# A gMLP layer in fp32 on one core: second half of x loaded two steps later, weights fetched ahead of parts of h, one emptying of a queue removed

## The chip, the cores and the metric

The kernel runs on one core of one Trainium2 chip. The metric is device microseconds of that core for the whole program. A run is repeated, and the median of the repeats is shown; the profile is of one more execution, whose own time is given beside its span.

## The reference

With DEPTH = 1 only the first mixer runs, a gated MLP with a spatial mixing over chunks of 128 positions. x is 1024 x 2048, `w_in` is 2048 x 12288, `w_out` is 4096 x 2048, all float32.

```python
h = rmsnorm(x, a_norm)
z = h @ w_in                                   # 1024 x 12288
u, v, gate = jnp.split(z, 3, axis=-1)          # 4096 columns each
u = gelu(u)
v = rmsnorm(gelu(v), v_gain)
sv = einsum('gpq,nqgc->npgc', w_s, v) + b_s    # 8 groups of 512 columns, chunks of 128 rows
y = u * sv
x = x + (y * silu(gate)) @ w_out
return rmsnorm(x, final_norm)
```

## The kernel before

**Arithmetic.** Every matrix product keeps float32 accuracy with a fast matmul type: a matrix is split into a high and a low part (`split`, L90: ACT copies the high part `w_hi`, L92; DVE subtracts it to get the low part `w_lo`, L93), and each product is the sum of three matmuls (`mm3`, L104: high by high L106, high by low L107, low by high L108). The big products are cut into 2 x 2 blocks and computed with seven block products in place of eight (`A_OF`, `B_OF`, L20); many of these need the sum or difference of two weight blocks, a `w_sum` that DVE makes (`combine`, L116).

**Strips and steps.** The input projection goes over 12 strips of 1024 columns (four of v, then eight that pair 512 columns of u with the same of the gate), then the output projection follows. The program is one list of steps (L124 to L129), each some 24 matmuls of 128 x 128 by 512. Strip 0 makes h from x itself and writes its parts to DRAM; all others read these parts of h back. From strip 2 on, strips come in pairs, and products 2 and 5 of a pair are cut once more by the same scheme: these "deep" steps have 12 matmuls, read the parts `d_1h` to `d_7l`, and come first in each pair (`deep_stage`, L504). There are five such stages, at strips 2, 4, 6, 8 and 10.

**What is fetched when.** At the start of step i, `advance` (L491) calls `prefetch` for the steps up to LOADS = 3 steps ahead (a deep step counts half) and then `feed` for step i + 2, which makes the `w_sum` and the split on DVE and ACT. `prefetch` (L176) loads a step's weight blocks (`load_w`, issued at L156, tile `w_raw`) and behind them its two parts of h (L191, tiles `a_hi` and `a_lo`). All of these go through the one queue of SP, in program order, 512 KB each; a load waits there until its slot in a pool of 21 ("big") is free. In strip 0, `first_step` (L315) loads the second half of x (`load_x`, L287, tile `x_t`) in the same queue, one of eight blocks in each of the steps 2 to 9. POOL's queue writes the parts of h to DRAM and moves v and y.

**Small work between steps.** What has to be done to a finished product (activations on ACT, the multiplication by the gain on DVE, L351, and so on) is put in two lists, `soon` and `later`. `work(us)` (L262) takes from them after each step, as far as a budget goes. `work_all` (L268) empties both; it is called at the end of strip 1 (L677), when the last products of that strip are in the lists, and in the deep stage of strip 4 (L528).

Engines execute their own instructions in program order, so a `w_sum` that waits for its weights holds up every DVE instruction behind it.

Of the kernel before, what the change touches and what calls it, by code (L numbers as in the profile page):

```python
# [7 lines left out]
F32 = mybir.dt.float32  # L8
F32R = mybir.dt.float32r
# [27 lines left out]
def gmlp_kernel(ctx, tc, x, xT, g_in, w_in, gain, wsT, bsT, w_out, fnorm, out):  # L37
    nc = tc.nc
# [12 lines left out]
    AHEAD, LOADS = 2, 3  # L51
# [7 lines left out]
    def slot(tag, name, dt=F32):  # L59
        return main.tile([P, 2, C], dt, tag=tag, name=name, bufs=SLOTS[tag])  # L60

    def bank_set(n, name):

        return [ps.tile([P, 2, 512], F32, tag=f"set{n}_{t}", name=f"{name}_{t}") for t in range(2)]
# [59 lines left out]
    steps = [("in", s, p, j) for s in range(2) for p in (IN_ORDER if s else FIRST_ORDER) for j in range(JI)]  # L124
    for s in range(2, len(strips), 2):
# [7 lines left out]
    a_dram = {(p, j): [dram.tile([P, 2, HT], F32, tag=f"a{p}_{j}{l}", name=f"a{p}_{j}{l}") for l in "hl"]  # L133
              for p in IN_ORDER for j in range(JI)}

    d_dram = {(p, q): [dram.tile([P, 2, C], F32, tag=f"d{p}_{q}{l}", name=f"d{p}_{q}{l}") for l in "hl"]
              for p in DEEP for q in IN_ORDER}

    wraw, yraw, wparts, aparts = {}, {}, {}, {}
    hx = {}  # L140

    def load_w(step, block, us=None):
        kind, s, p, j = step
        mat, cols, n = (w_out, outs, JO) if kind == "out" else (w_in, strips, JI)

        key = (kind, s, 0 if kind == "in" and not (s > 1 and (p, block) == (6, 11)) else p, block, j)
        if key not in wraw or us is not None:
            k = ((block // 10 - 1) * n + j) * 2 * P
            col = cols[s][block % 10 - 1]
            if key not in wraw:  # L150
                wraw[key] = slot("big", "w_raw")

            order = "(p u) c -> p u c" if kind == "out" else "(u p) c -> p u c"
            src = mat[k:k + 2 * P, col:col + C].rearrange(order, p=P)
            us = slice(0, 2) if us is None else us
            nc.sync.dma_start(out=wraw[key][:, us], in_=src[:, us])  # L156
        return wraw[key]

    def load_deep(step, block):

        _, s, (p, q), j = step
        return load_w(("deep", s + block % 10 - 1, p, 2 * (block // 10 - 1) + j), 11 if p == 2 else 22)

    def load_y(step, block):
        _, _, p, j = step
        key = (p, block, j)
        if key not in yraw:
            g, b = divmod(((block % 10 - 1) * JO + j) * 2, CB)
            if g == G - 1 and halves_of_y[0] < 2 * G:
                work_all()  # L170
            yraw[key] = slot("big", "y_raw")
            nc.gpsimd.dma_start(
                out=yraw[key], in_=y_dram[g][block // 10 - 1][b * P:(b + 2) * P].rearrange("(p u) t -> p u t", p=P))
        return yraw[key]

    def prefetch(i):  # L176
        if i >= len(steps):
            return
        kind, s, p, j = step = steps[i]
        if kind == "deep":  # L180
            for block in B_OF[p[1]][::2]:
                load_deep(step, block)
        else:
            for block in B_OF[p][::2]:
                load_w(step, block)
        if kind == "deep" and j > 0:
            aparts[i] = aparts[i - 1]
        elif kind == "deep" or (kind == "in" and s > 0):
            parts = [slot("big", f"a_{l}", F32R) for l in ("hi", "lo")]
            for t, d in zip(parts, d_dram[p] if kind == "deep" else a_dram[p, j]):  # L190
                nc.sync.dma_start(out=t.bitcast(F32), in_=d)  # L191
            aparts[i] = parts
        if kind == "out" and s == 0:
            for block in A_OF[p][::2]:
                load_y(step, block)
# [66 lines left out]
    def work(us=2.3):  # L262
        while soon or (later and us > 0):
            cost, what = (soon or later).pop(0)
            us -= cost
            what()

    def work_all():  # L268
        while soon or later:
            work(1e9)  # L270
# [6 lines left out]
        out=eye, in_=ones[:, 0, :P], pattern=[[-1, P]], compare_op=ALU.is_equal, fill=0.0, base=0, channel_multiplier=1)  # L277
# [3 lines left out]
    def load_x(jj, h, us=None):  # L281

        if (jj, h) not in hx:
            hx[jj, h] = slot("ax" if h == 1 and jj >= JI else "big", "x_t")
        src = xT[jj * 2 * P:(jj + 1) * 2 * P, h * HT:(h + 1) * HT].rearrange("(u p) c -> p u c", p=P)
        us = slice(0, 2) if us is None else us
        nc.sync.dma_start(out=hx[jj, h][:, us], in_=src[:, us])  # L287

    def square_x(jj, h):

        sq = slot("ax", "sq_x")
        nc.scalar.activation(out=sq, in_=hx[jj, h], func=AF.Square)
        if h in sums:
            nc.vector.tensor_tensor(out=sums[h], in0=sums[h], in1=sq, op=ALU.add)
        else:
            sums[h] = sq
# [17 lines left out]

    def first_step(i):  # L315

        if 2 <= i < 10:
            load_x(i - 2, 1)
        if i == 4:
            nc.gpsimd.dma_start(out=ws_sb, in_=wsT.rearrange("g q p -> q g p"))  # L320
        if 1 <= i < 17:
            h, n = divmod(i - 1, 8)
            square_x(order_x[n] if h == 0 else n, h)
        if i in (9, 17):
            scale_x(i // 10)
        if i in (10, 20):

            for t in range(2):
                later.append((0, lambda t=t, act=waiting[i // 10]: act(t)))
# [9 lines left out]
    for j in range(1, JI):  # L339
        load_x(j, 0)  # L340
        load_x(JI + j, 0)
        if j < LOADS:
            prefetch(j)
# [57 lines left out]
    def spatial_step(k, g, cs, n_set):  # L401

        for c, at in enumerate((0, 1, 4, 5)):
            if k == at:
                load_v(g, c)
        for c, at in enumerate((2, 3, 6, 7)):
            if k == at:
                prepare_spatial(g, c)
        if k in (6, 10):
            work(0)  # L410
            half = k // 10
            apply_spatial(g, half, n_set[half], cs[11 + 10 * half])
# [73 lines left out]
    when = [0.0]  # L486
    for step in steps:
        when.append(when[-1] + (0.5 if step[0] == "deep" else 1.0))
    fetched, fed = [LOADS], [AHEAD]

    def advance(i):  # L491
        while fetched[0] < len(steps) and when[fetched[0]] <= when[i] + LOADS:
            prefetch(fetched[0])
            fetched[0] += 1
        feed(i + AHEAD)
# [5 lines left out]
    i = 0  # L501
    deep = {}
# [43 lines left out]
    for s in range(len(strips)):  # L546
# [7 lines left out]
        if is_v:  # L554
            gains = slot("ax", "gain_b")
            load_gains = lambda s=s, gains=gains: nc.gpsimd.dma_start(
                out=gains.rearrange("p a b -> p (a b)"),
                in_=gain[:, 2 * s * C:2 * (s + 1) * C].broadcast_to([P, 2 * C]))
# [90 lines left out]
        for p in FIRST_ORDER if s == 0 else IN_ORDER if s == 1 else REST_ORDER:  # L649
            fresh = p in (1, 2, 5) or (s > 1 and p in (4, 3))  # L650
            if s == 0:
                work(0)
            if fresh:
                second = (1,) if s == 0 else (2,) if s == 1 else (4,)
                sets[p] = bank_set(b if p in second else a, f"m{p}")
            chain = sets[p if fresh else {4: 2, 7: 2, 3: 5, 6: 5}[p] if s < 2 else {7: 4, 6: 3}[p]]
            for j in range(JI):
                advance(i)
                if is_v and (p, j) == (3, 0):
                    load_gains()  # L660
                if not is_v and p in (7, 6):
                    spatial_step(j if p == 7 else 4 + j, *mixing)
                elif p == 1 and s > NV and s % 2:
                    spatial_step(8 + j, *before)
                products(i, chain, fresh)
                if s == 1 and p in DEEP:
                    whole(i)
                if s == 0:
                    first_step(i)
                work(2.3 if s else 1.4)  # L670
                i += 1
            end_of(p, chain)
            if s == 1 and p in DEEP:
                for q in IN_ORDER:
                    later.append((2.3, lambda p=p, q=q: deep_parts(p, q)))
            if s == 1 and p == 6:
                work_all()  # L677
        before = mixing


# [60 lines left out]
    for p in OUT_ORDER:  # L741
        for s in range(len(outs)):
# [3 lines left out]
            for j in range(JO):  # L746
                if j == JO // 2:
                    for block, _ in TO_C[p]:
                        init_acc(s, block)
                    if p == OUT_ORDER[-2] and s == 1:  # L750
                        for n in range(2):
                            fn_b.append(slot("ax", f"fn_b{n}"))
                            nc.gpsimd.dma_start(
                                out=fn_b[n].rearrange("p a b -> p (a b)"),
                                in_=fnorm[:, 2 * n * C:2 * (n + 1) * C].broadcast_to([P, 2 * C]))
# [16 lines left out]
            if last:  # L772

                work_all()
                for m in range(HCH):
# [3 lines left out]
                    d = acc[s, block][m // 2][:, m % 2]  # L779
# [53 lines left out]
```

## Time and profile before

| | |
|---|---|
| median of 3 runs | 2497.97 us (2497.07 to 2501.28) |
| profiled execution, own time | 2498.71 us |
| its span | 2497.0 us |
| mean granted TensorE clock | 0.995 |
| PE busy | 2442.9 us, 98% of the span, 10708 matmuls |
| DVE busy | 1831.9 us, 73%, 1847 instructions |
| ACT busy | 986.1 us, 39%, 1236 instructions |
| DMA | 752.24 MB, mean 301 GB/s |
| loads of `w_in` blocks, 512 KB each | 311, median 7.1 us from issue to landing |

TensorE (PE) is busy nearly all the time, so what can be won is in the short stretches where it is not. The profile cuts the span into 40 slices of 62.4 us, a digit for the busy tenths of each; most digits of PE are 9. Behind it stand views of any stretch: counts and busy time by window, the instructions of one engine in order, the chain of waits, and what each engine waited for. SP and POOL only issue transfers here: "SPq" rows are issues, not the transfers themselves.

### The profile page before, as it was taken

The numbers are of one execution on the slowest core, as the hardware profiler recorded it, in microseconds if no ns is written. First come the engines' busy times: TensorE is split into PE (matmuls) and PEld (weight loads), VectorE is DVE, ScalarE is ACT, GpSimd is POOL, SyncE is SP. The second block draws the span as 40 slices with busy tenths as digits, with TensorE's granted clock in tenths as the row PEclk, the third lists the DMA queues.
The fourth block names the chain that finished last, engine by engine and source line by source line (L and its number), as shares of the span: only waits on it lengthen the run. The fifth ranks groups of instructions, "written<-read, shape, count | busy, mean of one in ns | idle before, by whom it ended". The sixth has DMA issues, their size and how long they took to land.

```text
span 2497.0 us, 29261 instructions
## 1 busy us (share of the span) xinstructions
PE 2442.9 (98%) x10708; PEld 2012.3 (81%) x10708; DVE 1831.9 (73%) x1847; ACT 986.1 (39%) x1236; POOL 234.8 (9%) x414
## 2 busy tenths in 40 slices
PE   8999979999999999999999999999999999999998
PEld 6778868888888887888878888788888888888886
DVE  6996768667876778867788677876777564676795
ACT  5853444333533344343443433434342332232343
POOL 2221100000000101001010010100102110010010
PEclk9999989999999999999999999999999999999999
DMA  9788898899988787897888878888798865678885
GB/s 381 269 335 284 329 381 328 291 346 341 345 311 333 271 328 286 310 340 272 335 288 296 334 278 320 300 304 328 280 339 301 303 221 187 215 275 279 303 278 204
DMA packets 276720, 752.24 MB, mean 301 GB/s; under 512 B 24784, under 2 KB 24800, under 8 KB 276576
## 3 DMA queue, kind: packets, MB, share of 16 engines
q1 hardware_dynamic: 231920, 593.57, 66.7%
q0 software_dynamic: 44656, 156.80, 16.6%
q8 instruction: 85, 1.39, 0.2%
q14 instruction: 59, 0.48, 0.1%
HBM read 664.29 MB, written 85.98 MB: 300 GB/s over the span
## 4 chain that ended last, share of the span: by engine, by line
PE 85%; DMA 7%; DVE 4%; issue 2%; ACT 1%; SPq 1%; POOL 0%; POOLq 0%; ACTq 0%; DVEq 0%
PE m L107 16%; PE m L108 16%; PE m L106 16%; PE o L107 7%; PE o L106 7%; PE o L108 7%; DMA w_raw<-in_w_in 5%; PE d L107 4%; PE d L108 4%; PE d L106 4%; DMA a_lo<-a_2l 1%; DVE w_lo L93 1%; DVE w_sum L116 1%; DMA x_t<-in_xT 1%; PE sv L107 1%
## 5 line engine op out<-in xcount | busy, mean ns | idle before, releaser
L92 ACT ACTIVATE w_hi<-w_sum 128x1024 fp32r<-128x1024 f32 x420 | 444.9, 1060 | 1068.8 <-PE m L107 645.7
L106 PE MATMUL m<-w_hi,a_hi 128*128 128x512 f32 x2048 | 799.2, 390 | 16.7 <-ACT a_hi L92 9.3
L107 PE MATMUL m<-w_lo,a_hi 128*128 128x512 f32 x2048 | 799.7, 391 | 8.4 <-DVE w_lo L93 8.4
L108 PE MATMUL m<-w_hi,a_lo 128*128 128x512 f32 x2048 | 798.6, 390 | 1.7 <-DVE a_lo L93 1.7
L93 DVE TENSOR_TENSOR w_lo<-w_sum,w_hi 128x1024 fp32r<-128x1024 f32 x420 | 513.0, 1221 | 274.4 <-ACT w_hi L92 272.5
L116 DVE TENSOR_TENSOR w_sum<-w_raw 128x1024 f32<-128x1024 f32 x420 | 511.3, 1221 | 198.6 <-DMA w_raw<-in_w_in 181.5
L106 PEld LDWEIGHTS m<-w_hi,a_hi 128*128 128x128 f32 x2048 | 385.3, 188 | 100.1 <-ACT a_hi L92 10.9
L107 PEld LDWEIGHTS m<-w_lo,a_hi 128*128 128x128 f32 x2048 | 385.6, 188 | 90.2 <-DVE w_lo L93 9.2
L108 PEld LDWEIGHTS m<-w_hi,a_lo 128*128 128x128 f32 x2048 | 385.4, 188 | 83.7 <-DVE a_lo L93 3.4
L106 PE MATMUL o<-w_hi,a_hi 128*128 128x512 f32 x896 | 348.7, 389 | 0.8 <-DVE o L780 0.8
L107 PE MATMUL o<-w_lo,a_hi 128*128 128x512 f32 x896 | 348.7, 389 | 0.7 <-DVE m_inv L87 0.7
L108 PE MATMUL o<-w_hi,a_lo 128*128 128x512 f32 x896 | 348.6, 389 | 0.0
L107 PE MATMUL d<-w_lo,a_hi 128*128 128x512 f32 x560 | 219.7, 392 | 16.4 <-DVE w_lo L93 16.4
L106 PE MATMUL d<-w_hi,a_hi 128*128 128x512 f32 x560 | 218.6, 390 | 0.0
L108 PE MATMUL d<-w_hi,a_lo 128*128 128x512 f32 x560 | 218.6, 390 | 0.0
L106 PEld LDWEIGHTS o<-w_hi,a_hi 128*128 128x128 f32 x896 | 168.2, 188 | 36.5 <-DVE o L780 1.5
L107 PEld LDWEIGHTS o<-w_lo,a_hi 128*128 128x128 f32 x896 | 168.2, 188 | 35.9 <-DVE w_lo L93 1.2
L108 PEld LDWEIGHTS o<-w_hi,a_lo 128*128 128x128 f32 x896 | 168.2, 188 | 34.9
L92 ACT ACTIVATE w_hi<-w_raw 128x1024 fp32r<-128x1024 f32 (+1 forms) x89 | 93.1, 1048 | 187.6 <-PE o L107 76.0
L93 DVE TENSOR_TENSOR w_lo<-w_raw,w_hi 128x1024 fp32r<-128x1024 f32 (+1 forms) x89 | 107.1, 1208 | 73.7 <-ACT w_hi L92 73.5
L429 POOL DMA_DIRECT2D y<-y_t x128 | 74.3, 588 | 713.3 <-DVE y_t L424 710.5
L107 PEld LDWEIGHTS d<-w_lo,a_hi 128*128 128x128 f32 x560 | 105.6, 189 | 41.5 <-DVE w_lo L93 19.8
(146 smaller groups left out, 1746.2 us busy)
## 6 DMA issues: line engine op xcount, KB each, us to landing
w_raw<-in_w_in SPq DMA_DIRECT2D x311, 512.0 KB, 7.1
w_raw<-in_w_out SPq DMA_DIRECT2D x192, 512.0 KB, 7.3
y_raw<-y POOLq DMA_DIRECT2D x96, 512.0 KB, 6.6
a_hi<-a_0h SPq DMA_DIRECT2D x57, 512.0 KB, 6.0
a_lo<-a_0l SPq DMA_DIRECT2D x57, 512.0 KB, 6.2
a_hi<-a_1h SPq DMA_DIRECT2D x57, 512.0 KB, 6.8
a_lo<-a_1l SPq DMA_DIRECT2D x57, 512.0 KB, 5.9
a_hi<-a_2h SPq DMA_DIRECT2D x57, 512.0 KB, 6.5
```

The costliest lines, as they stand in the source:

```text
L92: nc.scalar.activation(out=hi, in_=raw, func=AF.Copy)
L93: nc.vector.tensor_tensor(out=lo, in0=raw, in1=hi.bitcast(F32), op=ALU.subtract)
L106: nc.tensor.matmul(out=acc, lhsT=ah, rhs=bh, start=start, stop=False, skip_group_check=on)
L107: nc.tensor.matmul(out=acc, lhsT=ah, rhs=bl, start=False, stop=False, skip_group_check=on)
L108: nc.tensor.matmul(out=acc, lhsT=al, rhs=bh, start=False, stop=stop, skip_group_check=on)
L116: nc.vector.tensor_tensor(out=s, in0=a, in1=b, op=ALU.add if of[1] > 0 else ALU.subtract)
L429: nc.gpsimd.dma_start(out=yd[n, :, :, q * P:(q + 1) * P], in_=yts[0][n][q * Q:(q + 1) * Q])
```

## The change

Three edits. First, in strip 0 the eight blocks of the second half of x are loaded in the steps 4 to 11, not 2 to 9. Second, `prefetch` is split: the new `prefetch_h` loads a step's parts of h, up to two steps ahead (LOADS - 1), and is called first in `advance`; `prefetch` keeps the weights and the loads of y, and reaches 3.5 steps ahead in deep steps and in the "in" steps of strips after the first, 3 elsewhere. Third, the call of `work_all` at the end of strip 1 is gone, so what is left in the lists is done in the steps that follow.

```diff
+    def prefetch_h(i):
+
+        kind, s, p, j = steps[i]
+        if kind == "deep" and j > 0:
+            aparts[i] = aparts[i - 1]
+        elif kind == "deep" or (kind == "in" and s > 0):
+            parts = [slot("big", f"a_{l}", F32R) for l in ("hi", "lo")]
+            for t, d in zip(parts, d_dram[p] if kind == "deep" else a_dram[p, j]):
+                nc.sync.dma_start(out=t.bitcast(F32), in_=d)
+            aparts[i] = parts
+
     def prefetch(i):
-        if i >= len(steps):
-            return
+
         kind, s, p, j = step = steps[i]
...
-        if kind == "deep" and j > 0:
-            aparts[i] = aparts[i - 1]
-        elif kind == "deep" or (kind == "in" and s > 0):
-            parts = [slot("big", f"a_{l}", F32R) for l in ("hi", "lo")]
-            for t, d in zip(parts, d_dram[p] if kind == "deep" else a_dram[p, j]):
-                nc.sync.dma_start(out=t.bitcast(F32), in_=d)
-            aparts[i] = parts
...
-        if 2 <= i < 10:
-            load_x(i - 2, 1)
+        if 4 <= i < 12:
+            load_x(i - 4, 1)
...
-    fetched, fed = [LOADS], [AHEAD]
+    fetched, fetched_h = [LOADS], [0]
 
     def advance(i):
-        while fetched[0] < len(steps) and when[fetched[0]] <= when[i] + LOADS:
+
+        while fetched_h[0] < len(steps) and when[fetched_h[0]] <= when[i] + LOADS - 1:
+            prefetch_h(fetched_h[0])
+            fetched_h[0] += 1
+        ahead = LOADS + 0.5 if steps[i][0] == "in" and steps[i][1] > 0 or steps[i][0] == "deep" else LOADS
+        while fetched[0] < len(steps) and when[fetched[0]] <= when[i] + ahead:
             prefetch(fetched[0])
             fetched[0] += 1
         feed(i + AHEAD)
...
-            if s == 1 and p == 6:
-                work_all()
```

What moves in SP's queue in the first strip is shown here, before the change. `w_raw` is a weight block, `x_t` a block of x; the number is the tile's own.

```order
L156 DMA w_raw_339<-in_w_in 128x2x512
L287 DMA x_t_379<-in_xT 128x2x512
L156 DMA w_raw_384<-in_w_in 128x2x512
L287 DMA x_t_424<-in_xT 128x2x512
L156 DMA w_raw_433<-in_w_in 128x2x512
L287 DMA x_t_474<-in_xT 128x2x512
L156 DMA w_raw_480<-in_w_in 128x2x512
L287 DMA x_t_520<-in_xT 128x2x512
L287 DMA x_t_567<-in_xT 128x2x512
L156 DMA w_raw_525<-in_w_in 128x2x512
L287 DMA x_t_614<-in_xT 128x2x512
```

The same places of the queue after the change (tiles are numbered anew: `w_raw_476` is what `w_raw_480` was, `w_raw_521` what `w_raw_525` was):

```order
L156 DMA w_raw_339<-in_w_in 128x2x512
L156 DMA w_raw_382<-in_w_in 128x2x512
L156 DMA w_raw_429<-in_w_in 128x2x512
L290 DMA x_t_470<-in_xT 128x2x512
L156 DMA w_raw_476<-in_w_in 128x2x512
L290 DMA x_t_516<-in_xT 128x2x512
L156 DMA w_raw_521<-in_w_in 128x2x512
L290 DMA x_t_563<-in_xT 128x2x512
L156 DMA w_raw_568<-in_w_in 128x2x512
L290 DMA x_t_610<-in_xT 128x2x512
L290 DMA x_t_661<-in_xT 128x2x512
```

Each block of x stands two places later, `w_raw_480` two and `w_raw_525` three places earlier.

The second place is SP's queue at the start of the first deep stage (strip 2), before the change; the `d_` tensors are the parts of h for its seven products, in the order 1, 2, 5, 4, 3, 7, 6.

```order
L156 DMA w_raw<-in_w_in 128x2x512 x2
L191 DMA a_hi<-d_1h 128x1024
L191 DMA a_lo<-d_1l 128x1024
L156 DMA w_raw<-in_w_in 128x2x512 x2
L191 DMA a_hi<-d_2h 128x1024
L191 DMA a_lo<-d_2l 128x1024
L191 DMA a_hi<-d_5h 128x1024
L191 DMA a_lo<-d_5l 128x1024
L156 DMA w_raw<-in_w_in 128x2x512
L191 DMA a_hi<-d_4h 128x1024
L191 DMA a_lo<-d_4l 128x1024
L156 DMA w_raw<-in_w_in 128x2x512 x2
```

And after it:

```order
L156 DMA w_raw<-in_w_in 128x2x512 x4
L184 DMA a_hi<-d_1h 128x1024
L184 DMA a_lo<-d_1l 128x1024
L184 DMA a_hi<-d_2h 128x1024
L184 DMA a_lo<-d_2l 128x1024
L184 DMA a_hi<-d_5h 128x1024
L184 DMA a_lo<-d_5l 128x1024
L156 DMA w_raw<-in_w_in 128x2x512 x3
L184 DMA a_hi<-d_4h 128x1024
L184 DMA a_lo<-d_4l 128x1024
```

The first two weight blocks and the first one of the second lot keep their places; the second pair of the first lot, and the pair for product 4's second half and product 3, stand two places earlier, and the parts `d_1` and `d_4` two places later. The other four deep stages have the same two shifts.

The third place is DVE in the same stage, before the change; `u` and `c` are results of strip 1, `gain_b` the gain.

```order
L93 TENSOR_TENSOR w_lo<-w_sum,w_hi 128x1024
L351 TENSOR_TENSOR c_1_2548<-c_1_2548,gain_b 128x512
L116 TENSOR_TENSOR w_sum<-w_raw 128x1024
L93 TENSOR_TENSOR w_lo<-w_sum,w_hi 128x1024
L116 TENSOR_TENSOR w_sum<-w_raw 128x1024 x2
L643 TENSOR_TENSOR u_1700<-u_1700,m_0_1842 128x1024
L643 TENSOR_TENSOR u_1701<-u_1701,m_1_1843 128x1024
L93 TENSOR_TENSOR w_lo<-w_raw,w_hi 128x1024
L351 TENSOR_TENSOR u_1700<-u_1700,gain_b 128x512 x2
L351 TENSOR_TENSOR u_1701<-u_1701,gain_b 128x512 x2
L93 TENSOR_TENSOR w_lo<-w_raw,w_hi 128x1024 x3
```

And after it:

```order
L93 TENSOR_TENSOR w_lo<-w_sum,w_hi 128x1024
L354 TENSOR_TENSOR c_1_2544<-c_1_2544,gain_b 128x512
L116 TENSOR_TENSOR w_sum<-w_raw 128x1024 x2
L93 TENSOR_TENSOR w_lo<-w_sum,w_hi 128x1024
L116 TENSOR_TENSOR w_sum<-w_raw 128x1024
L651 TENSOR_TENSOR u_1696<-u_1696,m_0_1838 128x1024
L651 TENSOR_TENSOR u_1697<-u_1697,m_1_1839 128x1024
L93 TENSOR_TENSOR w_lo<-w_raw,w_hi 128x1024 x2
L354 TENSOR_TENSOR u_1696<-u_1696,gain_b 128x512 x2
L93 TENSOR_TENSOR w_lo<-w_raw,w_hi 128x1024
L354 TENSOR_TENSOR u_1697<-u_1697,gain_b 128x512 x2
L93 TENSOR_TENSOR w_lo<-w_raw,w_hi 128x1024
```

One `w_sum` (for product 4's second half) now stands ahead of the `w_lo` of product 1's second half, and the four multiplications of `u` by the gain are spread between the next `w_lo`. PE executes the same instructions in the same order as before, and so does POOL.

## Rows read from the trace of the kernel before

**Rows 1.** Windows of 50 us: busy time (count) by engine, clock, DMA share, GB/s.

```profile
50.00:100.00 50.00, 44.58 (x190) 34.97 (x188) 44.05 (x50) 36.51 (x50) 9.87 (x16) 1.00 0.81 296
...
200.00:250.00 50.00, 50.00 (x222) 41.41 (x221) 33.11 (x34) 16.54 (x18) 5.31 (x10) 1.00 0.81 287
```

**Rows 2.** Timeline of PE, first strip: start, duration, instruction, [idle before, releaser].

```profile
60.59 0.50 PE L106 MATMUL m<-w_hi,a_hi 128*128 128x512 f32 x1 [1.56 <-ACT c L630]
...
65.86 0.50 PE L106 MATMUL m<-w_hi,a_hi 128*128 128x512 f32 x1 [2.93 <-ACT c L630]
```

**Rows 3.** Timeline of DVE, the same stretch.

```profile
53.75 1.23 DVE L116 TENSOR_TENSOR w_sum<-w_raw 128x1024 f32<-128x1024 f32 x1 [1.17 <-DMA w_raw<-in_w_in]
...
56.03 1.22 DVE L218 TENSOR_TENSOR a_sum<-x_t 128x1024 f32<-128x1024 f32 x1
...
62.58 1.23 DVE L116 TENSOR_TENSOR w_sum<-w_raw 128x1024 f32<-128x1024 f32 x1 [2.87 <-DMA w_raw<-in_w_in]
```

**Rows 4.** Timeline of SP's queue, the same stretch: issues.

```profile
24.66 3.12 SPq L156 DMA_DIRECT2D w_raw<-in_w_in  x1
...
29.48 1.14 SPq L156 DMA_DIRECT2D w_raw<-in_w_in  x1
...
55.01 0.37 SPq L156 DMA_DIRECT2D w_raw<-in_w_in  x1
```

**Rows 5.** DMA issues of 24 to 32 us: count, KB, median us to landing.

```profile
w_raw<-in_w_in SPq DMA_DIRECT2D x2, 512.0 KB, 22.6
```

**Rows 6.** Windows of 5 us at the first deep stage, columns as in Rows 1.

```profile
340.00:345.00 5.00, 5.00 (x24) 4.13 (x23) 4.46 (x5) 2.25 (x4) 1.07 (x2) 1.00 1.03 418
...
355.00:360.00 5.00, 2.72 (x6) 2.15 (x7) 4.03 (x5) 5.00 (x13) 0.20 (x1) 0.50 1.03 413
```

**Rows 7.** Timeline of PE at the first deep stage.

```profile
330.37 0.80 PE L107 MATMUL m<-w_lo,a_hi 128*128 128x512 f32 x1 [6.97 <-DVE w_lo L93]
...
357.28 0.79 PE L107 MATMUL d<-w_lo,a_hi 128*128 128x512 f32 x1 [8.50 <-DVE w_lo L93]
```

**Rows 8.** Timeline of DVE at the first deep stage.

```profile
327.96 1.22 DVE L116 TENSOR_TENSOR w_sum<-w_raw 128x1024 f32<-128x1024 f32 x1 [13.46 <-DMA w_raw<-in_w_in]
...
341.42 0.69 DVE L351 TENSOR_TENSOR c<-c,gain_b 128x512 f32<-128x512 f32 x1
...
351.47 2.36 DVE L116 TENSOR_TENSOR w_sum<-w_raw 128x1024 f32<-128x1024 f32 x2 [6.78 <-DMA w_raw<-in_w_in]
353.75 2.34 DVE L643 TENSOR_TENSOR u<-u,m 128x1024 f32<-128x1024 f32 x2
356.01 1.22 DVE L93 TENSOR_TENSOR w_lo<-w_raw,w_hi 128x1024 fp32r<-128x1024 f32 x1
```

**Rows 9.** Timeline of SP's queue at the first deep stage.

```profile
331.86 0.32 SPq L191 DMA_DIRECT2D a_lo<-d_4l  x1
```

**Rows 10.** DMA issues of 329 to 334 us.

```profile
a_lo<-d_4l SPq DMA_DIRECT2D x1, 512.0 KB, 15.3
```

**Rows 11.** Chain of waits, 295 to 370 us: start, duration, what.

```profile
298.99 20.31 DMA a_lo<-a_2l
...
333.17 18.21 DMA w_raw<-in_w_in
...
358.50 0.43 PE d L106
```

**Rows 12.** What PE waited for, whole span: total us, times, longest.

```profile
PE d L107 <- DVE w_lo L93: 16.4, 7, 8.5
```

**Rows 13.** The same, 985 to 1000 us.

```profile
PE d L107 <- DVE w_lo L93: 2.5, 2, 1.4
```

**Rows 14.** Timeline of DVE at the deep stage of strip 6.

```profile
988.74 1.23 DVE L116 TENSOR_TENSOR w_sum<-w_raw 128x1024 f32<-128x1024 f32 x1 [4.05 <-DMA w_raw<-in_w_in]
```

**Rows 15.** Timeline of SP's queue at the same stage.

```profile
974.54 0.38 SPq L191 DMA_DIRECT2D a_hi<-d_5h  x1
```

**Rows 16.** DMA issues of 974.4 to 979 us.

```profile
a_hi<-d_5h SPq DMA_DIRECT2D x1, 512.0 KB, 8.7
```

## The prediction, made blind

> **What bounds the kernel now.** I read the windows of 50 us first, to see where TensorE (PE) loses time. Undisturbed it starts 222 matmuls in 50 us, one per 0.225 us [rows 1], and nothing but PE's own rate bounds these windows, which are most of the span. Fewer start in the first strip (190 in one window [rows 1]), at the first deep stage, and a little fewer at the deep stages of strips 6, 8 and 10. Then I read PE's timeline there, for the idle time before a matmul and its releaser, and behind the releaser DVE's and SP's timelines, for the transfer that came last.
>
> All the stalls that the change can touch have one form: a `w_sum` on DVE waits for a weight block, and the split that PE needs is behind it. In the first strip PE idles 1.56 and 2.93 us [rows 2], while DVE idles 1.17 and 2.87 us before two `w_sum`, released by `w_raw` [rows 3]. At the first deep stage PE idles 6.97 and 8.50 us [rows 7], and DVE 13.46 and 6.78 us for the same reason [rows 8]. PE idles in deep products seven times for 16.4 us in the whole span; without the 8.50 that leaves 7.9 us in six stalls [rows 12], which lie in pairs at strips 6, 8 and 10 (2.5 us at strip 6 [rows 13]).
>
> DVE as a whole is no bound; these are late transfers. SP issues in order, and a block lands about when the queue ahead of it has landed: at the first deep stage the DMA engines are full (share 1.03, 418 GB/s [rows 6]) and 512 KB take 15.3 to 20.31 us from issue to landing [rows 10, 11], against a median of 7.1 us over the kernel. So what counts is a block's place in SP's queue. The change makes no load larger and adds none; it trades places. My estimate is to give each block the landing time that its new place had before.
>
> **First strip.** The two blocks of the two waits stand two and three places earlier. The first, issued at 29.48 and landed just before 53.75 [rows 3, 4], takes the place of the block issued at 24.66. The two have a median of 22.6 us to landing [rows 5], and 53.75 less 29.48 is some 24.3, so the other took about 20.9 and landed at 45.6; DVE is free for it at 53.75 - 1.17 = 52.58. The second was issued only at 55.01 [rows 4], when a slot came free, and now has the place that lands before 53.75; DVE wants it at 62.58 - 2.87 = 59.71 at the earliest, less the 1.17 won before. Both DVE waits go: 1.17 + 2.87 = 4.0 us. DVE has work without a gap in between [rows 3], so PE, which waited behind it for 4.49 us, gets about 4.0 us of that.
>
> Late instead could be the second half of x. The block in the old place 22 is pushed behind a weight block that lands ahead of 53.75; the `a_sum` that reads it starts at 56.03 [rows 3], now 1.2 earlier, at 54.9. That is a margin of one us, the thinnest of the four such blocks. If the blocks of x land late by as much as the weights did, nothing is won: bounds 0 and 4.5, and I take 4.0, since the places give it.
>
> **First deep stage.** The first stall (6.97) stays. Its `w_sum` [rows 8] reads one of the blocks at the head of the stage's queue, and these keep their places, behind the same loads. The second stall ends when three things are through on DVE: the `w_sum` of product 3, two adds of `u`, and the `w_lo` that PE waits for. Before, the two late `w_sum` start at 351.47 and the `w_lo` ends at 356.01 + 1.22 = 357.23 [rows 8]; PE starts at 357.28 [rows 7]. The latest block was issued from 333.17 on and took 18.21 us and a little more [rows 11]. Product 3's block now has the place of the low part of `d_4`, issued at 331.86 and landed 15.3 us later, at 347.2 [rows 9, 10]. One `w_sum` (half of 2.36), the adds (2.34) and the `w_lo` (1.22) [rows 8] bring PE to 347.2 + 1.2 + 2.3 + 1.2 = 351.9: 5.3 us earlier. The other `w_sum` now stands ahead of the `w_lo` before, so some of the remaining 3 us of stall moves one product forward; that is in the 351.9.
>
> The clock is the other half. After the stall of 8.50 the granted clock was 0.50 (that is 1.2 of 2.4 GHz) in one window [rows 6] and eight matmuls of the chain took 0.43 us each [rows 11], not 0.225: 8 x 0.2 = 1.6 us. With the stall cut to about 3 us in two pieces I expect the full clock, as the window with the 2.93 us of the first strip shows 1.00 [rows 1, 2]. Together 6.9 us, bounds 0 and 8.50 + 1.6 = 10.1.
>
> [...]
>
> **Deep stages of strips 6, 8, 10.** At strip 6 the first late block now has the place of the high part of `d_5`, issued at 974.54 and landed 8.7 us later, at 983.2 [rows 15, 16]. DVE waited for it from 988.74 - 4.05 = 984.69 [rows 14], so this wait goes whole, and with the second block two places up as well, so does the second. The queue is the same at strips 8 and 10, with transfers up to a us slower. I take the whole 7.9 us [rows 12]; bounds 0 (the block lands no earlier) and 7.9.
>
> **Parts of h.** They stand two places later, and are asked for two steps ahead of use where it was three. `d_4` is the nearest: it lands now when the late weights did, at 333.17 + 18.21 = 351.4 or a us later [rows 11]. PE reads it four deep steps, or 48 matmuls (10.8 us [rows 1]), after the matmul that started at 357.28, now 351.9: at 362.7. The margin of 10 us is the cover; bounds 0 and the rival below. In plain strips the loads stand in the queue as before.
>
> **`work_all`.** Without it DVE does the four multiplications of `u` (0.69 us each [rows 8]) between the next splits rather than together, and ACT its activations. They are 2.8 us of DVE beside deep products of 2.7 us PE time that need one split each (1.2): hidden, so nothing; bounds 2.8 either way, as they sit just behind the stall.
>
> **Sum.** 4.0 + 6.9 + 7.9 = 18.8 us. The profiled execution took 2498.71 (its span 2497.0, and 1.7 around it): 2479.9. The median of the runs is 0.74 lower: 2479.2.
>
> **Rivals.**
> (1) The order in SP's queue buys nothing at the first deep stage, because the DMA engines are full there [rows 6] and the late blocks wait for bytes in front of them, some of them POOL's. For it: share 1.03. Against it: between issues at 331.86 and 333.17, landing differs by 4 us [rows 9 to 11], so place does count. The `w_sum` then holds up the product before, and the 6.9 us are not won: 2486.1. This is what the Trainium skill makes of it ("DMA: Bandwidth & Descriptors", section "Issuing engines are not separate DMA queues"): transfers of all issuers run on the same 16 engines and interleave. The rows agree that they are full, and no run here shows a reorder.
> (2) The blocks of x come late in the first strip, the margin being one us, and the 4.0 us are not won: 2483.2.
> (3) The first stall goes too (6.97, and about 1.6 of slow clock as after the other), if the queue ahead of it drains sooner: 2479.2 - 8.6 = 2470.6. Against it: the same places hold.
> (4) The change doesn't do what it says: each load waits for a free slot, which DVE and PE give back at the same times as before, and the landings follow the slots and not the places. Then the stalls stay: 2498. For it: the block issued at 55.01, which had waited for its slot [rows 4]. Against it: the late blocks were issued 18 to 24 us before they landed [rows 4, 5, 11]; their time went in transfer.
> (5) Slower: parts of h come late. They are asked for two steps ahead, 48 matmuls or 10.8 us [rows 1], and at the worst of the burst one took 20.31 us [rows 11]. If SP reaches them only then, PE waits 20.3 - 10.8 = 9.5 us in each of the five deep stages, 47 us, against 18.8 won: 2479.2 + 47 = 2526. It decides for slower where more than 4 us per stage are lost. Against it: SP runs ahead of PE, and issued `d_4` at 331.86, 25 us before the stall's end.
>
> **Numbers.** Forecast, 2474 to 2486 for itself: 0.55. Rival 1: 0.13. Rival 2: 0.09. Rival 3: 0.07. Rival 4, no change: 0.10. Rival 5: 0.06. The range goes down to rival 3 and a little (2468) and up past rival 1 and the mults' bound (2489); outside lie rivals 4 and 5, 0.16. A measurement of this kernel can tell about 0.2%, 5 us, from no change. Rivals 1 to 3 are all faster by more than that, so faster 0.84, same 0.10, slower 0.06.
>
> **What would show it.** In PE's timeline after: the idle before the matmuls at about 60 and 65 us gone; the 6.97 still there; the 8.50 split into two of 1 to 2 us with the clock at 1.00 after them; no idle of PE behind `w_lo` at strips 6, 8 and 10. In DVE's: no wait for `w_raw` of over 2 us but the one before the first deep stage. The prediction is wrong if PE waits for a load of h (releaser `a_hi` or `a_lo` with a DMA), if an `a_sum` waits for `x_t`, or if `w_raw` in the deep stages lands no earlier than before.

## The result: 17 us faster, as forecast, and the profile after

Measured: 2481.71 us, the median of 4 runs (2480.11 to 2486.14), against 2499.19 for the kernel before beside it. The ratio is 0.993, 95% interval 0.9917 to 0.9942, so 17.5 us less, give or take 3. The forecast was 2479.2 (2468 to 2489). The profiled execution took 2480.11, its span 2478.4, against 2497.0 before: 18.6 us.

The first strip. PE's timeline there, the stretch of [rows 2]:

```profile
58.43 0.50 PE L106 MATMUL m<-w_hi,a_hi 128*128 128x512 f32 x1 [0.24 <-ACT c L638]
```

And DVE's, which answers to [rows 3]:

```profile
51.66 1.22 DVE L116 TENSOR_TENSOR w_sum<-w_raw 128x1024 f32<-128x1024 f32 x1
52.79 1.22 DVE L297 TENSOR_TENSOR sq_x<-sq_x 128x1024 f32<-128x1024 f32 x1
53.93 1.22 DVE L221 TENSOR_TENSOR a_sum<-x_t 128x1024 f32<-128x1024 f32 x1
...
57.53 1.22 DVE L116 TENSOR_TENSOR w_sum<-w_raw 128x1024 f32<-128x1024 f32 x1
```

The two `w_sum` have no bracket any more: DVE did not wait for them. PE's 1.56 us became 0.24, and the 2.93 us are gone (0.04 left). No `a_sum` waits for its block of x either.

The first deep stage, PE [rows 7]:

```profile
325.76 0.79 PE L107 MATMUL m<-w_lo,a_hi 128*128 128x512 f32 x1 [6.33 <-DVE w_lo L93]
...
343.73 0.50 PE L107 MATMUL d<-w_lo,a_hi 128*128 128x512 f32 x1 [1.63 <-DVE w_lo L93]
...
349.70 0.50 PE L107 MATMUL d<-w_lo,a_hi 128*128 128x512 f32 x1 [2.95 <-DVE w_lo L93]
```

DVE at the same place [rows 8]:

```profile
323.34 1.23 DVE L116 TENSOR_TENSOR w_sum<-w_raw 128x1024 f32<-128x1024 f32 x1 [14.03 <-DMA w_raw<-in_w_in]
324.48 1.22 DVE L93 TENSOR_TENSOR w_lo<-w_sum,w_hi 128x1024 fp32r<-128x1024 f32 x1
...
341.31 1.22 DVE L116 TENSOR_TENSOR w_sum<-w_raw 128x1024 f32<-128x1024 f32 x1 [2.43 <-DMA w_raw<-in_w_in]
342.45 1.22 DVE L93 TENSOR_TENSOR w_lo<-w_sum,w_hi 128x1024 fp32r<-128x1024 f32 x1
345.03 1.23 DVE L116 TENSOR_TENSOR w_sum<-w_raw 128x1024 f32<-128x1024 f32 x1 [1.35 <-DMA w_raw<-in_w_in]
346.17 2.35 DVE L651 TENSOR_TENSOR u<-u,m 128x1024 f32<-128x1024 f32 x2
348.43 1.22 DVE L93 TENSOR_TENSOR w_lo<-w_raw,w_hi 128x1024 fp32r<-128x1024 f32 x1
```

The first stall stays, and the 8.50 us became 1.63 and 2.95, each behind a `w_sum` that waits. After them the clock stayed up. Windows of 5 us [rows 6]; the clock is the column behind POOL's:

```profile
325.00:330.00 5.00, 4.24 (x10) 3.37 (x11) 5.00 (x7) 3.13 (x6) 0.53 (x1) 0.50 1.03 409
...
350.00:355.00 5.00, 5.00 (x23) 4.11 (x22) 3.91 (x5) 5.00 (x10) 0.53 (x1) 1.00 1.04 402
```

What PE waited for, whole span [rows 12]:

```profile
PE d L107 <- DVE w_lo L93: 5.5, 4, 2.9
...
PE m L108 <- DMA a_lo<-a_0l: 0.8, 1, 0.8
```

Less the 1.63 and 2.95, the three late deep stages together keep 1.0 us of 7.9. The second row is new, a part of h that PE waits for, once, at 286.7 us in strip 1.

DVE's own waits in the late deep stages did not all go. Of the two at strip 6 one is left, and it is longer than the 1.78 us that it was before:

```profile
981.96 1.23 DVE L116 TENSOR_TENSOR w_sum<-w_raw 128x1024 f32<-128x1024 f32 x1 [3.60 <-DMA w_raw<-in_w_in]
983.10 1.22 DVE L93 TENSOR_TENSOR w_lo<-w_sum,w_hi 128x1024 fp32r<-128x1024 f32 x1
```

Strips 8 and 10 keep one of 3.33 and one of 3.12 us. PE is behind these waits for 0.62, 0.34 and 0.14 us only.

### The profile page after: what moved, and what is told of

Its sections match the earlier page's. It is cut to its first block, busy times and chain, and to the rows that moved or that the text cites. A ratio compares the mean times of both kernels' runs of the same rounds, so it can differ in the third digit from the quotient of the medians.

```text
span 2478.4 us, 29265 instructions
## 1 busy us (share of the span) xinstructions
PE 2440.5 (98%) x10708; PEld 2011.7 (81%) x10708; DVE 1831.9 (74%) x1847; ACT 985.9 (40%) x1236; POOL 234.0 (9%) x414
## 4 chain that ended last, share of the span: by engine, by line
PE 88%; DMA 6%; issue 3%; DVE 2%; ACT 1%; POOL 1%; SPq 0%; POOLq 0%; ACTq 0%; DVEq 0%
PE m L106 16%; PE m L107 16%; PE m L108 16%; PE o L106 8%; PE o L107 8%; PE o L108 8%; PE d L107 4%; PE d L108 4%; PE d L106 4%; DMA w_raw<-in_w_in 3%; DMA a_hi<-a_2h 1%; DMA x_t<-in_xT 1%; DVE w_lo L93 1%; PE sv L106 1%; PE sv L108 1%
```

## The experiments

Each run is compared with the kernel before, measured beside it on the same chip; its median there was 2499.1 to 2500.1 us.

**Each edit alone.** The second half of x only:

```diff
-        if 2 <= i < 10:
-            load_x(i - 2, 1)
+        if 4 <= i < 12:
+            load_x(i - 4, 1)
```

> The kernel before with one edit: the second half of x is loaded in the steps 4 to 11. Theory (the parts of the change add up, each acting through a weight block's place in the queue): the first strip alone is shorter by about 4.2 us, both waits of DVE for w_raw at 53 and 62 us are gone, the stalls of 6.97 and 8.50 us at the first deep stage and the six of the later ones stay; in all 4 us faster, ratio 0.9983. Rival (the parts of the change need each other: a faster first strip only brings the first deep stage earlier to a burst that ends when it ends): the 4 us are lost again in the stalls at 330 us, which grow, and the time is that of before within 1 us.

Measured: 2495.36, ratio 0.9983 (0.9974 to 0.9991): 4.2 us. In its trace PE's two waits are 4.2 us shorter, but 1.0 us is lost just behind them: a third weight block comes later, DVE waits 1.52 us for it at 71.44 us (0.52 before), and PE 1.23 us for the sum of squares of x (0.23 before). In the runs with this edit that wait of PE goes from 0.22 to 1.23 us. All later stalls stand. The parts add up here; the rival falls.

The split of the fetching only (`prefetch_h` and the new `advance`, the rest as before):

```diff
+        while fetched_h[0] < len(steps) and when[fetched_h[0]] <= when[i] + LOADS - 1:
+            prefetch_h(fetched_h[0])
+            fetched_h[0] += 1
+        ahead = LOADS + 0.5 if steps[i][0] == "in" and steps[i][1] > 0 or steps[i][0] == "deep" else LOADS
-        while fetched[0] < len(steps) and when[fetched[0]] <= when[i] + LOADS:
+        while fetched[0] < len(steps) and when[fetched[0]] <= when[i] + ahead:
```

> The kernel before with the second edit alone: parts of h fetched by themselves two steps ahead, weights half a step further ahead. Theory: the second stall of the first deep stage falls from 8.50 to some 5 us in two pieces and its slow clock goes, and the six stalls of the later deep stages fall from 7.9 us to 1 or 2: 5.9 + 7.8 less 1.1 for a part of h that comes late in strip 1, so 12 to 13 us faster, ratio 0.995. Rival (the gain of the deep stages comes from the queue of VectorE not being emptied): 4 us or less.

Measured: 2488.47, ratio 0.9957 (0.9944 to 0.9969): 10.7 us, 2 less than expected. In its trace the later deep stages are 7.8 us shorter, as expected, but the first one 2.2 and not 5.9. Its two stalls are 1.95 and 1.41 us, the clock fell behind the first (0.68 in the window of 350 to 355 us, which cost some 1.9 us), and two new stalls of PE come right behind them:

```profile
359.32 0.50 PE L106 MATMUL d<-w_hi,a_hi 128*128 128x512 f32 x1 [0.93 <-ACT w_hi L92]
360.58 0.50 PE L107 MATMUL d<-w_lo,a_hi 128*128 128x512 f32 x1 [0.76 <-DVE w_lo L93]
```

ACT in that run, ahead of the `w_hi` that PE waits for:

```profile
353.31 2.56 ACT L574 ACTIVATE u<-u,rx 128x512 f32<-128x512 f32 x4 [7.76 <-DVE u L651]
355.78 0.62 ACT L353 ACTIVATE sq_v<-u 128x512 f32<-128x512 f32 x1
...
357.62 0.62 ACT L353 ACTIVATE sq_v<-u 128x512 f32<-128x512 f32 x1
...
358.23 1.04 ACT L92 ACTIVATE w_hi<-w_raw 128x1024 fp32r<-128x1024 f32 x1
```

These four squares are what `work_all` emptied into the queue at once; without it two of them stand behind this `w_hi` and two behind the next. The first strip has the old queue here, and its stall of 3.70 us was followed by the low clock too (0.51 in the window of 65 to 70 us, some 2.4 us), which the trace of the kernel before, with 2.93 us there, doesn't show. So how the 2 us divide among these stays open.

`work_all` removed, nothing else:

```diff
-            if s == 1 and p == 6:
-                work_all()
```

> The kernel before with the third edit alone: work_all at the end of strip 1 is not called. Theory: no change, within 1 us, the stall of 8.50 us still ends with the same w_lo, since the two adds of u and the late w_sum still stand ahead of it. Rival: the four multiplications by the gain and the activations stood in the way behind the stall, and 2 to 3 us are won.

Measured: 2500.22, ratio 1.0002 (0.9993 to 1.0011). Nothing, as costed. Put back in the changed kernel (the same two lines with +; the 1.09 and 1.03 us of the expectation are the 0.93 and 0.76 shown above):

> The changed kernel with the call of work_all at the end of strip 1 put back. Theory (the third edit counts only once the late transfers are gone: with the lists emptied at once, ACT's activations and squares stand ahead of the w_hi of product 2, which cost 1.09 and 1.03 us of idle PE when the split of the queues was run alone): 2 us slower than the changed kernel, 2483.5 to 2484.5. Rival (the third edit does nothing here either, as it did nothing alone): within 0.5 us of the changed kernel.

Measured: 2483.13, ratio 0.9934 (0.9922 to 0.9947). Its interval and that of the changed kernel (0.9917 to 0.9942) overlap, so whether the third edit is worth 1 or 2 us beside the others stays open. The squares do stand ahead of the `w_hi` in this trace too, but PE idles 0.41 us there, not 2.

**Place in the queue, or lead in the program?** Three runs change one number of the changed kernel, how far ahead the parts of h are fetched (it is 2 steps there):

```diff
-        while fetched_h[0] < len(steps) and when[fetched_h[0]] <= when[i] + LOADS - 1:
+        while fetched_h[0] < len(steps) and when[fetched_h[0]] <= when[i] + LOADS:
```

> The changed kernel with the parts of h fetched three steps ahead, as in the kernel before; weights still half a step further ahead, x and work_all as changed. SP's queue at strips 6, 8 and 10 is then word for word that of before, though the program asks for each weight block half a step earlier; at the first deep stage the first two weight blocks stand two places later than before. Theory (the place in SP's queue decides, not how far ahead the program asks): the 7.9 us of idle PE at strips 6, 8 and 10 come back, the first stall grows by 2 or 3 us, 2495 to 2499, slower than the changed kernel by 14 us or more. Rival (asking half a step earlier is what brings the weights earlier): 2480 to 2485.

Measured: 2494.39, ratio 0.9976 (0.9967 to 0.9985), just under the range expected. What PE and DVE waited for:

```profile
DVE w_sum L116 <- DMA w_raw<-in_w_in: 205.2, 105, 11.0
PE d L107 <- DVE w_lo L93: 11.7, 7, 3.6
```

Less the 3.6 at the first deep stage, that is 8.1 us in six stalls, those of [rows 12] come back. The weights are asked for as early in the program as in the changed kernel and move the same bytes; at these strips SP's queue is that of before, instruction for instruction. DVE's order at them is that of before too, but for two `w_lo` per stage. So it is the place in the queue that counts, and with it the slot that a load gets, which these runs do not separate. Rival 1 of the prediction (a full DMA makes the order worthless at the first deep stage) falls with the stage itself: with the split alone its second stall, 8.50 us, became 1.95 and 1.41. The first two stalls sit elsewhere than expected (3.5 us behind a `w_hi` at 284 us and 4.6 at 336 in place of one larger one at 326); why wasn't followed up.

One step ahead (`when[i] + LOADS - 2`):

> The changed kernel with the parts of h fetched one step ahead, not two. Theory (SP runs far ahead of PE, so a part of h still lands before its use in the deep stages; only where its margin is gone already, in the burst at the end of strip 1, PE waits): 2 to 8 us slower than the changed kernel, 2484 to 2490, with PE waiting for a_hi or a_lo in strip 1 around 285 to 320 us. Rival 5 of the prediction (parts of h that come late in every deep stage decide): 9.5 us per stage and more, 2520 and above.

Measured: 2470.69, ratio 0.9884 (0.9869 to 0.99). Both expectations had the wrong sign: it is 11 us faster than the changed kernel. And in the step itself (`when[i] + LOADS - 3`):

> The changed kernel with the parts of h fetched in the step that uses them, with no lead at all. Theory (a lead in steps of the program is not a lead in time: SP runs ahead until a slot is missing, and what a smaller lead changes is only the place in SP's queue behind the weights): PE waits for parts of h of the late strips' first steps by one place each, some 1.3 to 2.5 us where the DMA engines are full; 2470 to 2480. Rival 5 of the prediction (a part takes 6 to 20 us from issue to landing, and PE stands still for it without a lead): 2600 and above, as 6 us are lost in most of 240 steps.

Measured: 2466.76, ratio 0.9871 (0.9854 to 0.9887), below even what the theory expected. The waits of this run:

```profile
DVE w_sum L116 <- DMA w_raw<-in_w_in: 18.5, 7, 9.2
PE d L107 <- DVE w_lo L93: 1.9, 2, 1.6
```

DVE's waits for weights go 205, 159, 57 and 18 us over the span as the parts of h go from 3 steps ahead to none, and PE waits for no part of h in the last. DVE's order differs in some places in these runs too. At the first deep stage it isn't the reason, for the late `w_sum` still stands ahead of the `w_lo` that PE needs:

```profile
313.96 1.23 DVE L116 TENSOR_TENSOR w_sum<-w_raw 128x1024 f32<-128x1024 f32 x1 [9.17 <-DMA w_raw<-in_w_in]
...
317.36 1.22 DVE L93 TENSOR_TENSOR w_lo<-w_sum,w_hi 128x1024 fp32r<-128x1024 f32 x1
```

The block landed 9.4 us earlier than in the changed kernel (323.34), and the stall of 6.33 us is gone. A part of h with no lead is still issued early: at the first deep stage SP issues `d_2` at 319.10, and PE uses it from 335.6 on. In the list of SP's own waits in this run most are for a slot (loads of weights wait 345 us, 98 times, for one that a `w_sum` gives back), fewer for a load that has yet to land (parts of h wait 31 us, 22 times, for a `w_raw`). So SP is held back by these, not by the step of the program that asks.

**Or DVE's order?** Here the first deep stage alone gets another order on DVE: each `w_sum` is queued behind the `w_lo` of one step before (first product) or two (the others). PE, SP and POOL are as in the changed kernel. ACT has two activations of `c` earlier.

```diff
+            lo_of[i] = split(raw[:, us], *[t[:, us] for t in wparts[i]])
...
-            raw = combine(B_OF[p[1]], lambda b: load_deep(step, b), "sum", "w_sum")
+            with tc.issue_after(lo_of[i - (1 if (s, p) == (2, (2, 1)) else 2)].ins) if s == 2 else nullcontext():
+                raw = combine(B_OF[p[1]], lambda b: load_deep(step, b), "sum", "w_sum")
```

> The changed kernel with another order on DVE at the first deep stage alone: each w_sum of that stage is issued behind the w_lo of the step before it (first product) or two before (the others), so that it no longer stands ahead of a split that PE needs sooner. SP, POOL and PE have the same instructions in the same order. Theory (what is left there is a w_sum that waits for its weights at the head of DVE's queue while a split that is ready stands behind it): the 6.49, 1.79 and 3.11 us go, with the slow clock after the first of them, 9 to 12 us faster than the changed kernel, about 2469 to 2472. Rival (the transfers are late for the products that use them too, the DMA engines being full): PE stalls at the deep products themselves for the same sum, and the time stays at 2480 to 2482.

Measured: 2469.83, ratio 0.9881 (0.9866 to 0.9897), 12 us faster than the changed kernel. (The 6.49, 1.79 and 3.11 us of the expectation are the stalls of 6.33, 1.63 and 2.95 in the trace.) DVE in this run:

```profile
316.02 1.23 DVE L93 TENSOR_TENSOR w_lo<-w_sum,w_hi 128x1024 fp32r<-128x1024 f32 x1 [0.26 <-ACT w_hi L92]
325.91 1.23 DVE L116 TENSOR_TENSOR w_sum<-w_raw 128x1024 f32<-128x1024 f32 x1 [8.66 <-DMA w_raw<-in_w_in]
327.05 3.69 DVE L357 TENSOR_TENSOR c<-c,gain_b 128x512 f32<-128x512 f32 x6
330.67 1.22 DVE L93 TENSOR_TENSOR w_lo<-w_sum,w_hi 128x1024 fp32r<-128x1024 f32 x1
```

ACT, for the same block:

```profile
327.23 1.06 ACT L92 ACTIVATE w_hi<-w_sum 128x1024 fp32r<-128x1024 f32 x1 [6.95 <-DVE w_sum L116]
```

And PE:

```profile
329.90 0.47 PE L106 MATMUL d<-w_hi,a_hi 128*128 128x512 f32 x1 [0.50 <-DMA a_hi<-d_1h]
...
331.94 0.65 PE L107 MATMUL d<-w_lo,a_hi 128*128 128x512 f32 x1 [1.56 <-DVE w_lo L93]
```

The weights still land late, at 325.9, and DVE still waits 8.66 us. But the `w_lo` that PE needs next is through before that wait, at 316 and not 324.48, and the 6.33 us are gone. The 1.56 us that are left are DVE's order again, not the late block: its `w_hi` is done at 327.23 + 1.06 = 328.3, but six multiplications by the gain stand between the `w_sum` and its `w_lo`. Without them the `w_lo` could end at some 329.5 (an estimate from these rows), before PE begins to wait at 330.4.

The same order in all deep stages (the condition `s == 2` taken away):

> The changed kernel with the order of the run before (w_sum behind the split of two steps before) in all five deep stages, not the first alone. Theory (a w_sum at the head of DVE's queue is what is left at strips 6, 8 and 10 as well): the 0.8, 0.5 and 0.3 us of idle PE there go, 1 to 2 us faster than with the first stage alone, about 2468. Rival (a w_sum that comes later makes its own split late, since w_sum, w_hi and w_lo take 3.5 us one after the other and a deep step 2.7): new stalls of 0.5 to 1 us at the products that use a w_sum, 5 to 15 us slower than with the first stage alone.

Measured: 2468.54, ratio 0.9877 (0.9863 to 0.989): 1.3 us better than the first stage alone by the medians, inside both intervals. The new stalls that the rival expected are 0.56 and 0.38 us at the first stage, and none at the later ones.

And the same order in the kernel before, without any of the three edits:

> The kernel before, none of the three edits, with DVE's order alone changed: in all deep stages each w_sum is issued behind the split of two steps before (of one step before for the first product of the first stage). SP, POOL and PE as before. Theory (the weights came late for DVE's order, not for the product that uses them): nearly all of the 20 us that the first deep stage loses goes but 2 to 3, and the 7.9 us of the later ones: 2474 to 2478, more than the change itself won. Rival (the transfers are late by themselves and only an earlier place in SP's queue helps): 2495 to 2500, as PE then stalls at the products that use the late weights.

Measured: 2476.87, ratio 0.9907 (0.9893 to 0.992). SP, POOL and PE execute the same instructions in the same order as in the kernel before; DVE's order changes, and a few activations of ACT move with it. That wins 22 us, at least as much as the change. What is left of the first deep stage in it:

```profile
335.47 0.50 PE L107 MATMUL d<-w_lo,a_hi 128*128 128x512 f32 x1 [2.28 <-DVE w_lo L93]
...
346.15 0.49 PE L106 MATMUL d<-w_hi,a_hi 128*128 128x512 f32 x1 [0.79 <-ACT w_hi L92]
```

Here too six multiplications by the gain (3.69 us from 330.59 on) stand between the late `w_sum` and the `w_lo` behind the 2.28 us.

**Both together.** The order in all stages and the parts of h one step ahead:

> The changed kernel with both: parts of h fetched one step ahead, and DVE's order (w_sum behind the split of two steps before) in all deep stages. Theory (what is left with the order alone is 2.5 us before the first deep product, whose weights land at about 323 us, and with the parts of h one step ahead these land some 3 us earlier): 2465 to 2467, with no stall of PE over 1 us between 170 us and the end of the last strip. Rival (the same stalls, counted twice): no faster than the better of the two, 2468 to 2470.

Measured: 2466.66, ratio 0.9872 (0.9857 to 0.9887). As expected, with one stall of 0.9 us for a part of h (`d_4`), and no better than no lead at all with the old order. The interval overlaps that of the order alone (0.9863 to 0.989), so that both together beat it is not shown. With the order in the first stage alone:

> As the run with both, but DVE's order in the first deep stage alone. Theory (with the parts of h one step ahead the later deep stages have no stall left, so the order changes nothing there): the same time as with the order in all stages, within 1 us. Rival (the order matters there too): 1 to 2 us slower than with all stages.

Measured: 2466.36, ratio 0.9872 (0.9857 to 0.9887): the same. Three ways end at 2466.4 to 2466.8, and all of them leave the deep stages with 0.9 to 2.1 us of stalls; what PE still loses lies mostly in the first 160 us (some 16 us) and behind its last matmul (some 9). They beat both kernels, by some 32 and 15 us.

## Why the prediction was right, point by point

- **First strip, 4.0.** Right: 4.2 us between the same two matmuls of the two traces (PE's 190th and 250th), and 4.2 when run alone. The blocks of x kept their thin margin. The sum has no term for the third weight block, which cost up to 1.0 us in other runs with the edit, and nothing in this trace.
- **First deep stage, 6.9.** The mechanism was right (first stall stays, second shrinks into two, the full clock after it), the size a little high: from the same matmul before the stage to the same one behind it, the stage became 5.9 us shorter. The term that was mis-sized is the landing of product 3's block. I took 15.3 us for its place; the chain of the changed kernel has 17.67:

```profile
327.26 17.67 DMA w_raw<-in_w_in
```

So the matmul behind these stalls started 3.6 us earlier, not 5.3. Behind it another 2.3 us came back, not 1.6: ten matmuls had been slow where I had counted eight, and the clock is most of it.

- **Later deep stages, 7.9.** 2.15, 3.18 and 2.43 us by the same count, 7.8. The sum is right, the reading of DVE half so: I had both of its waits go, and at each strip one stayed, of 3.1 to 3.6 us. At strip 6 its block landed 2.2 us earlier, but DVE, free of the first wait, came to it 4.0 us earlier. So DVE's wait grew while PE's stall shrank.
- **Parts of h, nothing.** Right for the deep stages. In strip 1, of which I had said that the queue stands as before, one part came late and cost 1.1 us in this trace. The run with DVE's order, whose queue is the same, shows no such wait, and neither does the one with `work_all` put back, so it is chance rather than the change.
- **`work_all`, nothing.** Right alone; beside the others open, by about 1.5 us.
- **What the sum didn't hold.** The start of the program was 0.8 us shorter (0.3 in the run with the first edit alone, whose queue there is the same) and the stretch of the output projection at 2430 us 1.0 (as much in the run with the first edit alone, which moves nothing there). 4.2 + 5.9 + 7.8 - 1.1 + 0.8 + 1.0 = 18.6, the difference of the spans. That this is so near the forecast's 18.8 is in part luck: without these two and the late part of h the terms make 17.9.
- **The signs.** Of those that I had named, two came out against the prediction: PE waited for a part of h (0.8 us, once), and DVE for `w_raw` for more than 2 us in the deep stages (2.43 at the first, 3.60, 3.33 and 3.12 at the later ones). PE lost little by them, so the sum stands, but as signs they were drawn too tightly: a wait of DVE counts only where PE is behind it.

Where the reasoning was short: I read the late transfer as the cause and DVE's order as given. The order experiment on the kernel before shows that it was as much the order: most of the late weights weren't late for the products that use them, only for a DVE that waited for them ahead of ready work. And rival 5 had the wrong sign for the lead: a smaller one made the kernel faster down to no lead at all.

## What to carry to other kernels

When an engine waits for a transfer, look at what is ready behind the waiting instruction: here the order on DVE alone won 22 us with the queue of loads untouched. When loads share one queue that runs ahead of its user, as SP's does here, a "lead" in steps is only a place in that queue. In this kernel it paid to give the front to the load with work between its landing and its use (weights that must be summed and split), and the rear to the one that is used as it lands (parts of h).

## What the runs showed of the hardware

The clock did not follow the length of the last stall. After 2.95 us of idle PE in the changed kernel the window kept 1.00 (above), and after 2.93 in the first strip of the kernel before it did too [rows 1, 2]. In the run with DVE's order, 0.50 and 1.56 us of idle, close behind each other, were followed by 0.53 (about 1.2 of 2.4 GHz). Windows of 2 us there:

```profile
330.00:332.00 2.00, 0.43 (x2) 0.12 (x2) 2.00 (x4) 0.00 (x0) 0.91 (x2) 1.00 1.02 406
332.00:334.00 2.00, 2.00 (x5) 1.62 (x6) 2.00 (x3) 0.89 (x1) 0.00 (x0) 0.53 1.03 420
```

With `work_all` put back, a stall of 2.88 us was followed by 0.66 in the window of 350 to 355 us, where the changed kernel has 1.00 after 2.95. With the order put into the kernel before, 2.28 us with no other stall close by were followed, four matmuls later, by 0.62 and 0.52 in the windows of 336 to 340 us. So what a short stall costs in clock can't be read off its length. By PE's cadence behind the stall (0.43 us a matmul in place of 0.23) each of these three falls cost some 1.7 us.
